# A weight tile's place in memory and the squares of x: two edits to a three-pass fp32r transformer block

## The chip, the cores and the metric

One core of a Trainium2 chip runs the kernel; its other engines are ScalarE (ACT), VectorE (DVE), GpSimd (POOL) and SyncE (SP, which issues transfers) beside TensorE (PE, with its weight loads as PEld). The metric is the device time of one execution in microseconds; three executions are shown. A profile, with its rows, comes from one further execution.

## The reference, cut to what matters

```python
h = rmsnorm(x, norm1_gain)                      # x: 512 positions x 2048
proj = h @ w_in                                 # 2048 x 7176, columns split among head groups
o_a = hgrn2_mixer(q_a, f_a, i_a, g_a, ...)      # 8 heads, chunked gated recurrence
o_b = fox_mixer(q_b, k_b, v_b, f_b, ...)        # 8 heads, forgetting attention
x = x + concatenate([o_a, o_b]) @ w_out         # 2048 x 2048
h = rmsnorm(x, norm2_gain)
x = x + (silu(conv3(h @ w_gate)) * (h @ w_up)) @ w_down    # 2048 x 5632, 5632 x 2048
y = rmsnorm(x, final_norm_gain)
```

The first norm needs, for each position, the sum of the squares of x over all 2048 features.

## The kernel before, in words

Everything is kept transposed: 128 features on the partitions, 512 positions along the row. Each fp32 operand is split into a high part in float32r (ScalarE copies it) and a low part, the rest (VectorE subtracts), and a product is made of three matmuls: high by high, low by high, high by low (`mms`, L211 to L213, and `v_unit`, L294 to L296).

The stages run one after the other. The **mixing stage** multiplies by w_in and runs the heads; the **output projection** multiplies by w_out; the **gate/up stage** multiplies by w_gate and w_up with half-width (256 column) matmuls on sums of quarter blocks (L832 to L834); the **down stage** multiplies by w_down. In the mixing stage, the output projection and the down stage the weights come through one `Stream`: SP loads 512 KB pieces called raw, `make` splits each half of a piece into whi (L159, ScalarE) and wlo (L160, VectorE), 512 columns each, and TensorE uses them in blocks of 128 columns. Two pieces are made ahead of use.

The **head** is the first `v_unit` (L345): its 16 blocks k of 12 matmuls each use one 128-row tile of x per block, loaded and split just before (`load_x`, L278; high part L228 on ScalarE, low part L229 on VectorE). In the head the activations are the stationary operand and the weights the moving one. `before(k)` loads two tiles of x ahead; `after(k)` puts the squares of x into the sum `acc1`: a square on ScalarE (L234 the first, L238 the others) and an addition (L239), which `after` gives to GpSimd. At k = 12 `rms_stats` starts; its matmuls L251 sum `acc1` over the partitions. A square and its addition are written at k = 4 to 11, but the scheduler that lays out each engine's queue issues what is ready first, and x is ready long before.

The heads' own work runs between the products of the projection, as generators that `step()` moves on after each product: per HGRN head four groups of small matmuls (L434; L442 to L452; L464 and L466; L474), per FoX head ten (L599; four times L211 to L213 or L614 on small tiles; four times L633; L656 to L658). `gates` (L573) multiplies by the weights of the forget gates, 40 columns a block, in 32 matmuls L577.

Where a tile lies follows from the order in which pools are opened. On the left lie small tiles, then the activations' pool `pa`, then raw (`wr`) and the weight parts (`wp`); on the right `po`, `px` and the forms of the gate/up stage. Tiles that only fill space set the offsets: `even` (EVEN floats), `even_cm` and `even_sm`, and, in the gate/up stage alone, `shift` (SHIFT = 16 floats, 64 bytes) ahead of the weight parts `wh` (L764, L765). So before the change the weight parts start at multiples of 512 bytes in all stages but gate/up, as the activations do in every stage; in gate/up they start 64 bytes past one.

Of the kernel before, what the change touches and what calls it, by code (L numbers as in the profile page):

```python
# [8 lines left out]
F32 = mybir.dt.float32  # L9
F32R = mybir.dt.float32r  # L10
I32 = mybir.dt.int32
AF = mybir.ActivationFunctionType
ALU = mybir.AluOpType
AX = mybir.AxisListType

P = 128
T = 512
D = 2048
KT = D // P
# [21 lines left out]
LEAD = 2  # L41
DMA_SUMS = True
SHIFT = 16
EVEN = 376
EVEN_CM = 24
EVEN_SM = 40

# [10 lines left out]
def tile_hymba_block(ctx: ExitStack, tc: tile.TileContext, xT, wst, wgu, wdn, wfb, consts, out, out_t):  # L58
    nc = tc.nc
    v, s, pe, gp = nc.vector, nc.scalar, nc.tensor, nc.gpsimd  # L60
# [3 lines left out]
    def opened(name, bufs, side="left", **kw):  # L64
        cm = tc.tile_pool(name=name, bufs=bufs, side=side, reuse_waits="tile", **kw)
        pools[name] = (cm, cm.__enter__())
        return pools[name][1]

    def closed(*names):
        for name in names:  # L70
            pools.pop(name)[0].__exit__(None, None, None)


    cp = opened("cp", 1)
    sm = opened("sm", 2)
    ev = opened("ev", 1)
    ev.tile([P, EVEN_SM], F32, name="even_sm")
    mm = opened("mm", 4, space=bass.MemoryType.PSUM)
    mx = opened("mx", 4, space=bass.MemoryType.PSUM)
    pa = opened("pa", 32)  # L80
    wr = opened("wr", 2)
    wp = opened("wp", 4)

    even = opened("even", 1, "right")
    even.tile([P, EVEN], F32, name="even")
    cm = opened("cm", 1, "right")
# [7 lines left out]
    def O(dt=F32, shape=(P, T)):  # L94
        return po.tile(list(shape), dt, name="ot", tag="o")
# [10 lines left out]
    def f32(ap):  # L106
        return ap.bitcast(F32)
# [28 lines left out]
    class Stream:  # L136
# [7 lines left out]
        def make(self):  # L144
            piece = self.made
            self.made += 1
            r, roff = divmod(piece * PIECE, RAW)
            if roff == 0:
                self.raw = self.wr.tile([P, RAW], F32, name="raw", tag="raw")
                width = PIECE if r == 0 else RAW  # L150
                for c in range(0, RAW, width):
                    nc.sync.dma_start(out=self.raw[:, c:c + width], in_=self.src[r, :, c:c + width])
            if self.pool is None:
                hi = self.wp.tile([P, PIECE], F32R, name="whi", tag="whi")
                lo = self.wp.tile([P, PIECE], F32R, name="wlo", tag="wlo")
            else:
                hi, lo = self.pool(F32R), self.pool(F32R)
            src = self.raw[:, roff:roff + PIECE]
            s.activation(hi, src, AF.Copy)  # L159
            v.tensor_tensor(lo, src, f32(hi), op=ALU.subtract)  # L160
            self.parts[piece] = (hi, lo)

        def piece(self, ahead):
# [11 lines left out]
        def four(self, ahead=AHEAD):  # L175
            hi, lo, _ = self.piece(ahead)
            self.n += 4
            return hi, lo

    ws = Stream(wst, NPIECE_A, wr, wp)  # L180


# [19 lines left out]
    def finish():  # L202
        while side:
            step()
# [27 lines left out]
    def square_acc(acc, src, first, eng=v):  # L232
        if first:
            s.activation(acc, src, AF.Square)  # L234
        else:
            sq = sm.tile([P, T], F32, name="sq", tag="sq")
            sq = sq[:, 0:src.shape[1]]
            s.activation(sq, src, AF.Square)  # L238
            eng.tensor_tensor(acc, acc, sq, op=ALU.add)  # L239
# [36 lines left out]
    acc1 = O()  # L276
# [61 lines left out]
            start(rms_stats([acc1], put1, 7))  # L338

    def after(k):  # L340
        for j in range(max(2 * k - 8, 0), min(2 * k - 6, KT)):
            square_acc(acc1, xs[j], j == 0, gp)

    xs = []
    vts = v_out(v_unit(True))  # L345
# [329 lines left out]
    dr = opened("dr", 1, space=bass.MemoryType.DRAM)  # L675
# [53 lines left out]
    def x1_out(d, ps):  # L729
        t = xr.tile([P, T], F32, name="xr", tag="xr")  # L730
        gp.dma_start(out=t, in_=xT[d * P:(d + 1) * P, :])
        v.tensor_tensor(t, t, ps, op=ALU.add)
        nc.sync.dma_start(out=x1d[d], in_=t)
        square_acc(acc2, t, d == 0)
        g = xr.tile([P, T], F32, name="hg", tag="hg", bufs=2)
        s.activation(g, t, AF.Copy, scale=con[:, C_G2 + d:C_G2 + d + 1])
        hg.append(g)
        if d % 2 and d < KT - 1:
            pair_forms(d // 2, hg[d - 1], hg[d])
# [4 lines left out]
    for d in range(WOPEN, KT):  # L744
        ps = MM()
        unit(ps, range(KT), os_)
        x1_out(d, ps)
    closed("wp", "wr", "pa")
    tl = opened("tl", 1)
    pair_forms(KP - 1, hg[-2], hg[-1])  # L750
    closed("xr")
# [8 lines left out]


    wf = opened("wf", 8)

    sh = opened("sh", 1)  # L764
    sh.tile([P, SHIFT], F32, name="shift")  # L765
    wh = opened("wh", LEAD + 2)
    gt = opened("gt", 1)
    ORDER = ("a11", "s2", "a12", "s3", "s1", "a22", "s4")
# [114 lines left out]
    closed("gt", "wh", "sh", "wf", "tl", "tt")  # L883


    wr = opened("wr", 3)
    wp = opened("wp", 4)
    pq = opened("pq", 81, "right")
# [110 lines left out]
            step()  # L999
        start(norm(i, ps, ys, 6 if i < 3 else 0))  # L1000
    finish()
    closed("pq", "wp", "wr", "even", "dr", "mx", "mm", "ev", "sm", "cp")


def _weights(w_in, w_out, w_gate, w_up, w_down):
# [70 lines left out]
```

## Time and profile before

| | us |
|---|---|
| three executions | 2253.15, 2252.39, 2254.7 (median 2253.15) |
| the profiled execution | 2252.45 |
| its span, first to last instruction | 2250.8 |
| TensorE busy | 2224.2 |
| VectorE busy | 1457.9 |
| ScalarE busy | 940.1 |
| GpSimd busy | 172.6 |

The mean granted clock of TensorE is 0.993 of its full 2.4 GHz. Matmuls overlap, so the duration of one is longer than the distance from its start to the next one's; where the text speaks of spacing, it means that distance. The profiled execution is 0.7 us below the median. The first projection starts at 6.0 us, the gate/up stage about 904 us, the down stage about 1751 us.

### The profile page before, as it was taken

To read this page: it belongs to the slowest core of one execution; us is meant where nothing else is said; L and a number is where in the kernel's file an instruction comes from. 1 tells how busy PE (TensorE), PEld (TensorE's weight loads), DVE (VectorE), ACT (ScalarE), POOL (GpSimd) and SP (SyncE) were. 2 spreads that over 40 slices of the span, in tenths; PEclk is the share of its full clock that TensorE was granted. 3 is DMA by queue.
4 is the path that set the end of the run, shared out by engine and by line. 5 is a ranking of instruction groups with operands and counts; after the bars stand their busy time and mean duration, and the time that the engine had idled before them with its cause. 6 is when DMAs were issued, how large, how long until landed. Compare 5 with 4: busy or idle time off the path is not lost. (4 is left out here: it accounts for less than half of the span.)

```text
span 2250.8 us, 34411 instructions
## 1 busy us (share of the span) xinstructions
PE 2224.2 (99%) x13662; PEld 1976.2 (88%) x13662; DVE 1457.9 (65%) x2194; ACT 940.1 (42%) x1484; POOL 172.6 (8%) x259
## 2 busy tenths in 40 slices
PE   8999999999999999999999999999999999999998
PEld 7888888788888887899999999999999788888886
DVE  6676467646457464888888888888888333333345
ACT  5333233234335354555555555555554222222234
POOL 5000000000000000100000000000000512000000
PEclk9999999999999999999999999999999999999999
DMA  5222222222222353888888888888885955332233
GB/s 179 86 85 76 94 85 89 75 88 81 85 85 75 113 169 129 246 224 222 229 214 222 226 223 224 221 221 224 223 220 145 383 205 201 99 98 99 89 103 113
DMA packets 112210, 352.67 MB, mean 157 GB/s; under 512 B 12816, under 2 KB 19088, under 8 KB 112048
## 3 DMA queue, kind: packets, MB, share of 16 engines
q1 hardware_dynamic: 89568, 272.67, 36.6%
q0 software_dynamic: 22336, 77.67, 15.9%
q8 instruction: 107, 1.75, 0.3%
q14 instruction: 55, 0.45, 0.1%
q10 hardware_dynamic: 144, 0.12, 0.0%
HBM read 318.96 MB, written 31.46 MB: 156 GB/s over the span
## 5 line engine op out<-in xcount | busy, mean ns | idle before, releaser
L160 DVE TENSOR_TENSOR wlo<-raw,whi 128x512 fp32r<-128x512 f32 x453 | 315.2, 697 | 453.8 <-ACT whi L159 415.4
L159 ACT ACTIVATE whi<-raw 128x512 fp32r<-128x512 f32 x453 | 284.5, 630 | 672.2 <-PE mxt L212 307.9
L820 ACT ACTIVATE fhi<-wq 128x1024 fp32r<-128x1024 f32 x308 | 328.0, 1066 | 334.2 <-PE pq L833 286.2
L821 DVE TENSOR_TENSOR flo<-wq,fhi 128x1024 fp32r<-128x1024 f32 x308 | 375.9, 1221 | 51.1 <-ACT fhi L820 50.0
L211 PE MATMUL mmt<-at,whi 128*128 128x512 f32 x896 | 354.7, 396 | 0.0
L213 PE MATMUL mmt<-at,wlo 128*128 128x512 f32 x896 | 349.7, 390 | 0.0
L212 PE MATMUL mmt<-at,whi 128*128 128x512 f32 x896 | 349.3, 390 | 0.0
L211 PE MATMUL mxt<-ot,whi 128*128 128x512 f32 x660 | 258.5, 393 | 3.0 <-ACT whi L159 2.7
L213 PE MATMUL mxt<-ot,wlo 128*128 128x512 f32 x660 | 257.9, 391 | 0.9 <-DVE wlo L160 0.9
L212 PE MATMUL mxt<-ot,whi 128*128 128x512 f32 x660 | 257.7, 391 | 0.2
L213 PEld LDWEIGHTS mmt<-at,wlo 128*128 128x128 f32 x896 | 168.1, 188 | 36.0
L211 PEld LDWEIGHTS mmt<-at,whi 128*128 128x128 f32 x896 | 168.3, 188 | 34.8 <-issue 1.9
L212 PEld LDWEIGHTS mmt<-at,whi 128*128 128x128 f32 x896 | 168.4, 188 | 32.9
L211 PEld LDWEIGHTS mxt<-ot,whi 128*128 128x128 f32 x660 | 124.5, 189 | 30.8 <-ACT whi L159 2.9
L212 PEld LDWEIGHTS mxt<-ot,whi 128*128 128x128 f32 x660 | 124.4, 189 | 27.6 <-DMA ot<-actd 1.6
L213 PEld LDWEIGHTS mxt<-ot,wlo 128*128 128x128 f32 x660 | 124.5, 189 | 26.7 <-DVE wlo L160 1.2
L778 POOL DMA_DIRECT2D wq<-wgu x88 | 75.9, 862 | 747.9 <-DVE flo L821 275.9
L796 DVE TENSOR_TENSOR wq<-wq 128x1024 f32<-128x1024 f32 x88 | 107.5, 1222 | 4.2 <-DMA wq<-wgu 2.6
L296 PE MATMUL mmt<-wlo,at 128*128 128x512 f32 x256 | 101.2, 396 | 3.7 <-DVE wlo L160 3.7
L294 PE MATMUL mmt<-whi,at 128*128 128x512 f32 x256 | 101.6, 397 | 0.9 <-ACT whi L159 0.9
L832 PE MATMUL pq<-b11h,fhi 128*128 128x256 f32 x352 | 98.4, 280 | 3.6 <-ACT fhi L820 3.6
L295 PE MATMUL mmt<-whi,at 128*128 128x512 f32 x256 | 100.7, 393 | 0.0
(303 smaller groups left out, 5032.7 us busy)
## 6 DMA issues: line engine op xcount, KB each, us to landing
wq<-wgu SPq DMA_DIRECT2D x220, 512.0 KB, 4.7
raw<-wst SPq DMA_DIRECT2D x143, 512.0 KB, 3.4
wq<-wgu POOLq DMA_DIRECT2D x88, 512.0 KB, 7.2
raw<-wdn SPq DMA_DIRECT2D x87, 512.0 KB, 3.4
ot<-actd POOLq DMA_DIRECT2D x88, 256.0 KB, 6.1
actd<-ah SPq DMA_DIRECT2D x44, 256.0 KB, 3.7
actd<-al SPq DMA_DIRECT2D x44, 256.0 KB, 3.1
xt<-xT SPq DMA_DIRECT2D x16, 256.0 KB, 5.3
```

Source lines behind the costliest of these rows:

```text
L159: s.activation(hi, src, AF.Copy)
L160: v.tensor_tensor(lo, src, f32(hi), op=ALU.subtract)
L211: pe.matmul(ps, lhsT=a, rhs=xh[:, ts], start=(first and i == 0), stop=False)
L212: pe.matmul(ps, lhsT=a, rhs=xl[:, ts], start=False, stop=False)
L213: pe.matmul(ps, lhsT=b, rhs=xh[:, ts], start=False, stop=(last and i == n - 1))
L294: pe.matmul(pss[i], lhsT=xh[:, ts], rhs=hi, start=(k == 0), stop=False)
L295: pe.matmul(pss[i], lhsT=xl[:, ts], rhs=hi, start=False, stop=False)
L296: pe.matmul(pss[i], lhsT=xh[:, ts], rhs=lo, start=False, stop=(k == KT - 1))
L796: v.tensor_tensor(t, raw[f, x], raw[f, y], op=ALU.add)
L820: s.activation(hi, t, AF.Copy)
L821: v.tensor_tensor(lo, t, f32(hi), op=ALU.subtract)
L832: pe.matmul(ps, lhsT=a, rhs=th, start=(first and j == 0), stop=False, **kw)
```

## The change

Weight parts: `shifted(n)` opens a pool with a tile of n floats that nothing uses. It is now opened after `pa` and ahead of `wr` and `wp` (16 floats, 64 bytes, for the mixing stage and the output projection), as before in the gate/up stage (16 floats), and ahead of `wr` and `wp` of the down stage (8 floats, 32 bytes). EVEN falls by 128 floats, so that all on the right lies 512 bytes higher. The last 44 weight parts of the down stage (`ws.pool = O`) come from the activations' pool and don't move.

Squares: 16 of them at k = 5 to 11, two or three a block, each square and its addition queued behind the last conversion (whi on ScalarE, wlo on VectorE) that was made by then; the addition is VectorE's.

```diff
-EVEN = 376
+SHIFT_D = 8
+EVEN = 248
+    def shifted(n):
+        opened("sh", 1).tile([P, n], F32, name="shift")
...
     pa = opened("pa", 32)
+    shifted(SHIFT)
     wr = opened("wr", 2)
     wp = opened("wp", 4)
...
-            s.activation(hi, src, AF.Copy)
-            v.tensor_tensor(lo, src, f32(hi), op=ALU.subtract)
+            queue_ends[:] = [s.activation(hi, src, AF.Copy),
+                             v.tensor_tensor(lo, src, f32(hi), op=ALU.subtract)]
...
     def after(k):
-        for j in range(max(2 * k - 8, 0), min(2 * k - 6, KT)):
-            square_acc(acc1, xs[j], j == 0, gp)
+        js = range(16 * (k - 5) // 7, 16 * (k - 4) // 7) if 5 <= k < 12 else []
+        if js:
+            with tc.issue_after(queue_ends[0].ins), tc.issue_after(queue_ends[1].ins):
+                for j in js:
+                    square_acc(acc1, xs[j], j == 0)
...
-    closed("wp", "wr", "pa")
+    closed("wp", "wr", "sh", "pa")
...
-    sh = opened("sh", 1)
-    sh.tile([P, SHIFT], F32, name="shift")
+    shifted(SHIFT)
     wh = opened("wh", LEAD + 2)
...
+    shifted(SHIFT_D)
     wr = opened("wr", 3)
     wp = opened("wp", 4)
```

Two places show how the queues change. The first is ScalarE in the head, from behind the first high part of x to the conversion of the third block of weights. Before (at is a high part of x, le belongs to the HGRN bounds, ot and sq are squares, whi_202 is the third block's):

```order
L234 ACTIVATE ot_128<-xt_135 128x512
L159 ACTIVATE whi_144<-raw_141 128x512
L159 ACTIVATE whi_172<-raw_141 128x512
L354 ACTIVATE le_596<-le_596 128x16
L228 ACTIVATE at_162<-xt_160,con_94 128x512
L238 ACTIVATE sq_277<-xt_160 128x512
L228 ACTIVATE at_168<-xt_166,con_94 128x512
L238 ACTIVATE sq_308<-xt_166 128x512
L228 ACTIVATE at_190<-xt_188,con_94 128x512
L228 ACTIVATE at_196<-xt_194,con_94 128x512
L238 ACTIVATE sq_311<-xt_188 128x512
L159 ACTIVATE whi_202<-raw_200 128x512
```

Now the same stretch of ScalarE's queue (whi_206 is the third block's, sel is a small constant):

```order
L365 ACTIVATE le_600<-le_600 128x16
L165 ACTIVATE whi_148<-raw_145 128x512
L165 ACTIVATE whi_176<-raw_145 128x512
L235 ACTIVATE at_166<-xt_164,con_98 128x512
L235 ACTIVATE at_172<-xt_170,con_98 128x512
L235 ACTIVATE at_194<-xt_192,con_98 128x512
L235 ACTIVATE at_200<-xt_198,con_98 128x512
L520 ACTIVATE sel_630<-ident_115 8x8
L521 ACTIVATE sel_630<-ident_115 8x8
L165 ACTIVATE whi_206<-raw_204 128x512
```

Four squares that stood ahead of the third block's whi stand behind it now.

The second place is VectorE in the head, around the conversions of the seventh block and later. Before (at is a low part of x here; no addition stands in this queue):

```order
L160 TENSOR_TENSOR wlo_293<-raw_258,whi_292 128x512
L229 SCALAR_TENSOR_TENSOR at_289<-xt_286,con_94,at_288 128x512
L229 SCALAR_TENSOR_TENSOR at_317<-xt_314,con_94,at_316 128x512
L229 SCALAR_TENSOR_TENSOR at_323<-xt_320,con_94,at_322 128x512
L160 TENSOR_TENSOR wlo_329<-raw_326,whi_328 128x512
```

Now, the additions into acc1 (ot_132) between them:

```order
L166 TENSOR_TENSOR wlo_293<-raw_262,whi_292 128x512
L236 SCALAR_TENSOR_TENSOR at_283<-xt_280,con_98,at_282 128x512
L236 SCALAR_TENSOR_TENSOR at_289<-xt_286,con_98,at_288 128x512
L246 TENSOR_TENSOR ot_132<-ot_132,sq_309 128x512
L236 SCALAR_TENSOR_TENSOR at_315<-xt_312,con_98,at_314 128x512
L236 SCALAR_TENSOR_TENSOR at_321<-xt_318,con_98,at_320 128x512
L166 TENSOR_TENSOR wlo_327<-raw_324,whi_326 128x512
L246 TENSOR_TENSOR ot_132<-ot_132,sq_342 128x512
L246 TENSOR_TENSOR ot_132<-ot_132,sq_345 128x512
```

The first addition comes after the sixth block's wlo (wlo_293), three stand by the seventh; the last of the 15 stands two conversions ahead of the sum over partitions.

## Rows read from the trace of the kernel before

**Rows 1.** The page, busy time of each engine, share of the span, instructions.
```profile
PE 2224.2 (99%) x13662; PEld 1976.2 (88%) x13662; DVE 1457.9 (65%) x2194; ACT 940.1 (42%) x1484; POOL 172.6 (8%) x259
```

**Rows 2.** Busy time by stretches: start:end, us, engines (xcount), granted clock, DMA, GB/s.
```profile
6.00:50.68 44.68, 40.98 (x165) 32.70 (x166) 34.09 (x37) 28.33 (x50) 26.42 (x29) 0.92 0.54 187
14.60:21.40 6.80, 5.47 (x13) 4.31 (x14) 6.80 (x5) 6.27 (x12) 5.75 (x5) 0.50 0.55 196
...
760.00:890.00 130.00, 130.00 (x576) 107.63 (x575) 77.96 (x154) 63.59 (x127) 7.72 (x15) 1.00 0.45 148
920.00:1740.00 820.00, 820.00 (x7237) 820.00 (x7237) 711.39 (x862) 430.85 (x518) 72.96 (x85) 1.00 0.82 219
1790.00:2100.00 310.00, 310.00 (x1370) 256.68 (x1369) 105.42 (x155) 72.06 (x114) 28.85 (x54) 1.00 0.42 148
```

**Rows 3.** Timeline of TensorE in the head: start us, us, what [idle before, releaser].
```profile
6.01 0.50 PE L294 MATMUL mmt<-whi,at 128*128 128x512 f32 x1 [0.90 <-ACT whi L159]
...
12.04 0.39 PE L294 MATMUL mmt<-whi,at 128*128 128x512 f32 x1
15.93 0.79 PE L296 MATMUL mmt<-wlo,at 128*128 128x512 f32 x1 [3.50 <-DVE wlo L160]
16.52 0.63 PE L295 MATMUL mmt<-whi,at 128*128 128x512 f32 x1
...
21.21 0.48 PE L294 MATMUL mmt<-whi,at 128*128 128x512 f32 x1
...
50.69 0.95 PE L251 MATMUL mxt<-ones,ot 128*128 128x1 f32 x8
```

**Rows 4.** Timeline of VectorE in the head.
```profile
9.39 4.71 DVE L229 SCALAR_TENSOR_TENSOR at<-xt,con,at 128x512 fp32r<-128x512 f32 x3
14.03 3.53 DVE L160 TENSOR_TENSOR wlo<-raw,whi 128x512 fp32r<-128x512 f32 x2
...
29.19 1.28 DVE L160 TENSOR_TENSOR wlo<-raw,whi 128x512 fp32r<-128x512 f32 x2
30.39 2.06 DVE L229 SCALAR_TENSOR_TENSOR at<-xt,con,at 128x512 fp32r<-128x512 f32 x3
```

**Rows 5.** Timeline of GpSimd in the head.
```profile
12.26 1.28 POOL L239 TENSOR_TENSOR ot<-ot,sq 128x512 f32<-128x512 f32 x1
...
14.04 4.66 POOL L239 TENSOR_TENSOR ot<-ot,sq 128x512 f32<-128x512 f32 x3
```

**Rows 6.** Groups from 4 to 45 us: shapes, xcount, busy us, mean ns, idle before.
```profile
L239 POOL TENSOR_TENSOR ot<-ot,sq 128x512 f32<-128x512 f32 x15 | 23.6, 1576 | 13.5 <-ACT sq L238 12.9
...
L228 ACT ACTIVATE at<-xt,con 128x512 fp32r<-128x512 f32 x16 | 11.2, 708 | 1.4 <-DMA con<-consts 1.4
L238 ACT ACTIVATE sq<-xt 128x512 f32<-128x512 f32 x15 | 9.2, 620 | 1.4 <-POOL ot L239 1.4
L159 ACT ACTIVATE whi<-raw 128x512 fp32r<-128x512 f32 x15 | 9.1, 624 | 10.6 <-DMA raw<-wst 5.5 <-PE mmt L295 3.3 <-DVE at L229 1.7
```

**Rows 7.** Timeline of TensorE after the small matmuls of the first HGRN head.
```profile
90.30 0.40 PE L212 MATMUL mmt<-at,whi 128*128 128x512 f32 x1
90.54 0.40 PE L213 MATMUL mmt<-at,wlo 128*128 128x512 f32 x1
...
91.01 0.39 PE L212 MATMUL mmt<-at,whi 128*128 128x512 f32 x1
...
92.39 0.39 PE L212 MATMUL mmt<-at,whi 128*128 128x512 f32 x1
```

**Rows 8.** Timeline of TensorE after a wait in the gate/up stage.
```profile
912.82 0.28 PE L832 MATMUL pq<-n2h,fhi 128*128 128x256 f32 x1
...
913.18 1.02 PE L271 MATMUL mxt<-dg,ones 128*128 128x512 f32 x2
```

**Rows 9.** Timeline of TensorE around the matmuls with the gate weights.
```profile
408.47 7.56 PE L577 MATMUL mmt<-at,ot 128*40 128x512 f32 x32
415.86 0.39 PE L294 MATMUL mmt<-whi,at 128*128 128x512 f32 x1
```

More of the change, by code (lines that the diff above doesn't have):

```diff
@@ L178, in four @@
             return hi, lo
+    queue_ends = []
     ws = Stream(wst, NPIECE_A, wr, wp)
@@ L1001, in tile_hymba_block @@
     finish()
-    closed("pq", "wp", "wr", "even", "dr", "mx", "mm", "ev", "sm", "cp")
+    closed("pq", "wp", "wr", "sh", "even", "dr", "mx", "mm", "ev", "sm", "cp")
 def _weights(w_in, w_out, w_gate, w_up, w_down):
```

## The prediction

> **What bounds the kernel now.** I read the page first: TensorE is busy for 2224.2 us, 99% of the span [rows 1], so only what lengthens TensorE's own chain counts. Second, the busy time by stretches [rows 2]. Each stretch divided by its matmuls gives a steady spacing: 820 us for 7237 matmuls in the gate/up stage is 113.3 ns for 256 columns. Twice that, 226.7 ns, is what 512 columns cost: 130 us for 576 in the output projection and 310 us for 1370 in the down stage are 226 ns. The gate/up stage already has its weight parts 64 bytes past the activations, the other two have no offset, and the spacing per column is the same. The exception is the head: 165 matmuls took 44.68 us where 165 x 0.2267 = 37.4 us would do, so 7.3 us are lost there. Part of it ran at a granted clock of 0.50, the 1.2 GHz level [rows 2].
>
> Third, the timeline of TensorE in the head [rows 3]. One matmul starts at 12.04 us and the next at 15.93 us, having waited for the low part wlo of the third block. After this idle time the clock is at 1.2 GHz: from 16.52 to 21.21 us 11 matmuls are 0.43 us apart instead of 0.227. That is 3.7 us of wait and about 2.6 us of slow clock (13 matmuls [rows 2] x 0.2 us); the other 1.0 us are two smaller waits for wlo and slightly wide spacings.
>
> Fourth, why wlo is late. VectorE alone makes two low parts of weights in 1.28 us and three of x in 2.06 us, some 0.69 us each [rows 4]. Between 9.39 and 17.56 us, though, three of x take 4.71 us and two of weights 3.53 us [rows 4], and in those microseconds GpSimd is adding squares [rows 5]. Normal would be 2.06 + 1.28 = 3.34 us; the row sums are 8.24 us. So GpSimd's adds, 15 of 1.58 us mean [rows 6], cost VectorE about 4.9 us up to 17.56 us, and 3.8 us of this lies ahead of the end of the third block's wlo (4.71 - 2.06 of the first three; 14.03 to about 15.9, when TensorE starts, less 0.69 of the next).
>
> **The change part by part.**
>
> Squares to VectorE. The GpSimd adds go (23.6 us of GpSimd work [rows 6]), and with them the stretching. The wlo of the third block would be there 3.8 us earlier, at 12.1 us. Two squares on ScalarE (0.62 us each [rows 6]) and a first one also leave the way of the third block's whi, so VectorE can start it earlier still. TensorE wants that wlo for its 28th matmul, at 6.01 + 27 x 0.227 = 12.1 us. The wait goes, and with no idle time the fall of the clock goes too.
>
> What comes in is 15 adds on VectorE at 0.69 us (a two-input pass over 128x512, like wlo), and 16 squares on ScalarE at a later place. Between block 2 and the sum over partitions at 50.69 us [rows 3], now some 32 us of TensorE time, VectorE must do 11 low parts of x, 13 of weights and 15 adds: 39 x 0.69 = 27 us. ScalarE must do 11 x 0.71 + 13 x 0.62 + 16 x 0.62 = 25.8 us [rows 6]. Both fit, with 5 us to spare, and the adds are queued behind the conversions of their own step, two blocks ahead of need. What would be late next is the sum of squares itself; it has those 5 us. I cost the new adds at nothing; uncovered they would cost at most 15 x 0.69 = 10.4 us. SP's queue keeps its order; GpSimd's two small DMAs lose three adds ahead of them, which nobody waits for.
>
> The first square now stands behind the first whi on ScalarE, not ahead of it, and TensorE's first matmul of the projection, at 6.01 us [rows 3], waits for that whi. This gains at most the square's 0.62 us. I set it against a few wide spacings that will stay, and take nothing. **Term 1: -7.3 us** (ends: -7.9 us, and -3.8 us if the clock still falls and some wait stays).
>
> Weight parts 64 bytes off in mixing stage and output projection. Here the trace shows only one thing that could be a matter of addresses. After each group of small matmuls the products of the projection do not fall back to 0.227 at once: from 90.30 to 92.39 us nine take 2.09 us instead of 2.04, some in pairs of 0.47 [rows 7]. Where weights lie 64 bytes off, in the gate/up stage, three spacings after a wait take 0.36 instead of 0.34 us and it is over [rows 8]. So 0.05 us per group would fall to 0.02. Groups: 4 per head in the HGRN heads (transposes, scores with states, outputs, mean of squares), 10 per head in the FoX heads (gate, four scores, four turns, output): 8 x 14 = 112. Upper end 112 x 0.05 = 5.6 us, lower end nothing. I take 0.03 us on two thirds of the groups, since in the FoX heads the next group often comes before nine products have passed: **term 2: -2.2 us**. I lean to the gate/up row because it is the one place with this very offset.
>
> A rule of the Trainium skill speaks against this term. SBUF — State Buffer, section "SBUF: two separate sides", says that within the engine side only the port pair shared by GpSimd and VectorE makes anyone wait, and that TensorE never does. By it the 64 and 32 bytes are worth nothing and the sum stops at term 1; the wide spacings of [rows 7] would then have a cause other than addresses, and no row here decides that.
>
> Weight parts 32 bytes off in the down stage. Its steady spacing is the 226 ns of [rows 2] and it has some dozen groups of small matmuls: a gain of at most 12 x 0.05 = 0.6 us. No row has this offset throughout. The nearest are 32 matmuls with the gate weights, whose blocks are 160 bytes apart, so that every second one starts 32 bytes past a multiple of 64: from 408.47 to 415.86 us they are 0.231 us apart and never reach 0.227 [rows 9]. For the 3 x 660 products of the down stage that would be 1980 x 0.0042 = +8.3 us. Against it: those loads have 40 columns, not 128, and the offset alternates. I take 0, from -0.6 to +8.3 us.
>
> The other moves: tiles on the right lie 512 bytes higher, alike modulo 512, and their padding shrinks. At the borders of the stages other tiles now share addresses; the built program's orders there do not change. Cost nothing; a first load that waits one product longer would be 24 x 0.113 = 2.7 us on a queue that TensorE may not feel.
>
> Sum: the profiled execution took 2252.45 us, 0.7 below the median of 2253.15. 2252.45 - 7.3 - 2.2 = 2242.95, and on the median **2243.6 us**.
>
> **The rivals.** About 0.2%, 4.5 us, is what a measurement of this kernel can tell from no change.
>
> (a) Addresses are worth nothing; only the head gains: 2253.15 - 7.3 = 2245.9 us. For it: the same spacing per column with and without offset [rows 2]. Against it: the quick recovery in [rows 8], though from few places. This is where the rule of the Trainium skill's page SBUF — State Buffer leads.
>
> (b) The head stays slow. VectorE or ScalarE fall behind through the adds between conversions, or the data of the first blocks come too late, and TensorE idles long enough for the clock to fall again: half the gain, 2253.15 - 3.7 = 2249.5 us, within the bound. Against it: 27 us of work in 32.
>
> (c) The 32 bytes spoil the down stage. If weights at half of 64 bytes keep the matmuls from their steady spacing, every product pays. At 0.231 us [rows 9] it is +8.3 us and the kernel ends at 2252 us, no change; at the 0.235 us of the wide pairs in [rows 7] it is 1980 x 0.0083 = +16.5 us, 2260 us, slower. It decides from a spacing of 0.2267 + (9.5 + 4.5) / 1980 = 0.2338 us on. Against it: a wide spacing has so far followed a disturbance, and hardly any disturb the down stage.
>
> (d) The 32 bytes help the steady spacing itself. 512 columns at 2.4 GHz would be 213.3 ns; the 13.4 ns over that on 1980 products are 26 us, and the time 2217 us. No row goes below 0.226 for 512 columns in a row, at any offset.
>
> **How the numbers follow.** Forecast (both terms) 0.50; (a) 0.28; (b) 0.10; (c) 0.10, of which 0.04 ends within the bound and 0.06 slower; (d) 0.02. Faster by over 0.2% are the forecast, (a), (d) and two of the ten of (b), where more than half of the gain comes: 0.82. Within: eight of (b) and four of (c), 0.12. Slower: 0.06. The range: the low end takes the upper bounds, -7.9 - 5.6 - 0.6, at 2239; the high end holds (a) and most of (b), 2250. Outside are (c), (d) and a little of (b).
>
> **What would show it.** In the changed profile: no adds on GpSimd; VectorE's wlo and low parts of x at 0.7 us throughout the head; the third block's wlo before 12 us; the clock at full level from the first matmul to the output projection's end; the sum over partitions at about 43.1 us instead of 50.69. For term 2: nine products after a group of small matmuls at 0.227 from the second or third on. For the down stage: 226 ns as before. I am wrong if TensorE still waits for wlo past 0.5 us in the head, if the down stage's matmuls per stretch change by over 1%, or if the time ends above 2250 us.

## The result, and the profile after

The changed kernel takes **2274.36 us** (median of four executions, 2273.93 to 2276.82) against 2252.83 us of the kernel before in the same comparison: a ratio of 1.0096, 95% interval [1.0079, 1.0114]. It is slower by 21.5 us. The forecast was 2243.6 us, faster by 9.5; the range of 2239 to 2250 does not hold the result. The profiled execution took 2274.59 us, with a span of 2272.9 us. Some executions of the kernel before and of some kernels below take 2278 to 2288 us, and in each of them that was profiled (e1, e8, e10, e12, e13; none of the kernel before) the gate/up products run at a second spacing; the comparison above has none of them.

TensorE is the bound as before, and it is busy longer: the page's busy times, beside [rows 1].

```profile
PE 2248.6 (99%) x13662; PEld 1974.1 (87%) x13662; DVE 1455.5 (64%) x2209; ACT 940.6 (41%) x1484; POOL 149.2 (7%) x244
```

The same 13662 matmuls cover 24.4 us more. The busy time by stretches of the changed kernel says where; the stretches are those of [rows 2], with the head's end moved to its new place.

```profile
6.00:44.14 38.14, 37.90 (x165) 30.80 (x165) 30.82 (x51) 28.60 (x50) 0.00 (x0) 1.00 0.60 218
14.60:21.40 6.80, 6.80 (x31) 5.58 (x30) 6.49 (x11) 6.52 (x13) 0.00 (x0) 1.00 0.86 333
...
760.00:890.00 130.00, 130.00 (x559) 104.19 (x558) 75.75 (x150) 62.09 (x124) 7.51 (x14) 1.00 0.46 150
...
1790.00:2100.00 310.00, 310.00 (x1331) 249.59 (x1330) 103.02 (x152) 69.56 (x111) 34.74 (x65) 1.00 0.43 154
```

The head needs 38.14 us for its 165 matmuls where it needed 44.68, and between 14.6 and 21.4 us, where 13 matmuls ran at a granted clock of 0.50, 31 now run at 1.00. But the same 130 us of the output projection hold 559 matmuls instead of 576, and the same 310 us of the down stage 1331 instead of 1370, with TensorE busy in all of both stretches and the clock at 1.00. No wait came in there. **A matmul of 512 columns starts later after the one ahead of it**: 130 us / 559 = 0.2326 us and 310 / 1331 = 0.2329. Read start to start in the steady part of these two stages, the mean spacing is 226.7 ns before and 233.3 ns after. The difference, 6.67 ns, is 16 cycles at 2.4 GHz.

The starts of the stages turn that into a balance. First the timeline of TensorE in the changed kernel, then in the kernel before, whose sum over partitions starts at 50.69 us [rows 3].

```profile
5.73 0.51 PE L301 MATMUL mmt<-whi,at 128*128 128x512 f32 x1 [0.41 <-ACT whi L165]
...
44.15 0.39 PE L258 MATMUL mxt<-ones,ot 128*128 128x1 f32 x3
...
913.87 0.58 PE L841 MATMUL pq<-b11h,fhi 128*128 128x256 f32 x1 [3.63 <-ACT fhi L829]
...
1760.34 0.50 PE L218 MATMUL mxt<-ot,whi 128*128 128x512 f32 x1 [2.67 <-ACT whi L165]
```

```profile
904.23 0.58 PE L832 MATMUL pq<-b11h,fhi 128*128 128x256 f32 x1 [3.63 <-ACT fhi L820]
...
1751.25 0.50 PE L211 MATMUL mxt<-ot,whi 128*128 128x512 f32 x1 [2.67 <-ACT whi L159]
```

| stretch | before, us | after, us | difference |
|---|---|---|---|
| start to the sum over partitions | 50.69 | 44.15 | -6.5 |
| from there to the gate/up stage | 853.54 | 869.72 | +16.2 |
| gate/up stage | 847.02 | 846.47 | -0.5 |
| down stage to the end of the span | 499.55 | 512.56 | +13.0 |
| span | 2250.8 | 2272.9 | +22.1 |

The waits at the two borders are the same in both (3.63 and 2.67 us). The gain of the head is there; 29 us came in, all in the stages where the weight parts were moved, and none in gate/up, where they stayed.

The 1980 products of the down stage at 6.67 ns make 13.2 us, which is its loss. The 16.2 us ahead of the gate/up stage have two prices. The 2688 products there with the weights stationary go from a mean of 227.6 ns to 233.3, 15.2 us: between the groups of small matmuls the kernel before runs above its 226.7 ns [rows 7], and the changed one is at 233.3 from the first product on. The 603 products behind the head that have the activations stationary and the weights moving go only from 227.5 to 229.4 ns, 1.1 us. Two rows of the changed kernel, nine spacings apart at the place of [rows 7], show the first kind:

```profile
90.29 0.39 PE L219 MATMUL mmt<-at,whi 128*128 128x512 f32 x1
...
92.39 0.39 PE L219 MATMUL mmt<-at,whi 128*128 128x512 f32 x1
```

A stretch of the second kind, in the kernel before and then in the changed one:

```profile
215.00:250.00 35.00, 35.00 (x156) 28.96 (x155) 13.77 (x18) 10.02 (x15) 0.53 (x1) 1.00 0.30 99
```

```profile
215.00:250.00 35.00, 35.00 (x155) 28.71 (x154) 12.53 (x17) 7.64 (x13) 0.53 (x1) 1.00 0.30 93
```

The head went as its step said. The timeline of VectorE in the changed kernel, where [rows 4] had 3.53 us for two low parts of weights and 4.71 us for three of x:

```profile
9.79 1.48 DVE L236 SCALAR_TENSOR_TENSOR at<-xt,con,at 128x512 fp32r<-128x512 f32 x2
11.66 1.29 DVE L166 TENSOR_TENSOR wlo<-raw,whi 128x512 fp32r<-128x512 f32 x2 [0.39 <-ACT whi L165]
12.87 2.73 DVE L236 SCALAR_TENSOR_TENSOR at<-xt,con,at 128x512 fp32r<-128x512 f32 x4
```

Two take 1.29 us and four 2.73, some 0.7 us each all through. The groups of the changed kernel from 4 to 45 us confirm it and give the price of the new adds:

```profile
L236 DVE SCALAR_TENSOR_TENSOR at<-xt,con,at 128x512 fp32r<-128x512 f32 x16 | 11.5, 748 | 1.5 <-ACT at L235 1.5
L166 DVE TENSOR_TENSOR wlo<-raw,whi 128x512 fp32r<-128x512 f32 x17 | 11.4, 685 | 4.7 <-ACT whi L165 4.7
...
L246 DVE TENSOR_TENSOR ot<-ot,sq 128x512 f32<-128x512 f32 x15 | 10.3, 688 | 0.6
```

The 15 adds cost 10.3 us of VectorE at 0.69 us each, as estimated. TensorE waits for none of them; ScalarE waits once, 0.3 us.

### The profile page after: what moved, and what is told of

It reads as the page before. It is cut to its first block, busy times and chain, and to the rows that moved or that the text cites. A ratio compares the mean times of both kernels' runs of the same rounds, so it can differ in the third digit from the quotient of the medians.

```text
span 2272.9 us, 34406 instructions
## 1 busy us (share of the span) xinstructions
PE 2248.6 (99%) x13662; PEld 1974.1 (87%) x13662; DVE 1455.5 (64%) x2209; ACT 940.6 (41%) x1484; POOL 149.2 (7%) x244
## 4 chain that ended last, share of the span: by engine, by line
PE 95%; DMA 2%; issue 1%; DVE 1%; ACT 0%; POOL 0%; SPq 0%; DVEq 0%; POOLq 0%; ACTq 0%
PE pq L842 11%; PE pq L843 11%; PE pq L841 11%; PE mmt L218 9%; PE mmt L219 9%; PE mmt L220 9%; PE mxt L219 7%; PE mxt L220 7%; PE mxt L218 7%; PE mmt L301 2%; PE mmt L303 2%; PE mmt L302 2%; DMA wq<-wgu 1%; DMA ot<-actd 1%; PE mxt L1006 0%
## 5 line engine op out<-in xcount | busy, mean ns | idle before, releaser
L218 PE MATMUL mmt<-at,whi 128*128 128x512 f32 x896 | 358.6, 400 | 0.0
L219 PE MATMUL mmt<-at,whi 128*128 128x512 f32 x896 | 353.7, 395 | 0.0
L218 PE MATMUL mxt<-ot,whi 128*128 128x512 f32 x660 | 262.6, 399 | 3.8 <-ACT whi L165 2.7
L219 PE MATMUL mxt<-ot,whi 128*128 128x512 f32 x660 | 261.8, 397 | 1.5 <-DMA ot<-actd 1.5
```

The costliest lines, as they stand in the source:

```text
L218: pe.matmul(ps, lhsT=a, rhs=xh[:, ts], start=(first and i == 0), stop=False)
L219: pe.matmul(ps, lhsT=a, rhs=xl[:, ts], start=False, stop=False)
```

## The experiments

Two theories stood after this. **Theory A:** the spacing depends on where the stationary block and the moving operand lie to each other, in bytes; the offset that is good for 256 moving columns is bad for 512. **Rival:** the spacing has to do with absolute places, with the stage, or with the other edit (the squares). e2 to e7, e9 and e15 have one execution each.

### The squares alone, and the offset undone by moving the activations too

e1: the change with the two new offsets taken out.

```diff
-EVEN = 248
+EVEN = 376
-    shifted(SHIFT)      # ahead of wr, wp of the mixing stage
-    shifted(SHIFT_D)
```

> The change without its offsets: weight parts of the mixing stage, output projection and down stage at multiples of 512 bytes as before, squares placed and added as in the change. Theory A (the offset of the weight parts costs 6.6 ns at each 512-column matmul, the squares are the gain): about 6.5 us under the kernel before, 2246 us, with the output projection and the down stage back at 226.7 ns a matmul and the sum over partitions at about 44.2 us. Rival (the later squares themselves cost the time further on): stays above 2260 us.

Seven executions took 2245.3 to 2249.8 us (median 2247.2), where twelve of the kernel before took 2252.4 to 2254.3 (median 2252.8): 5.6 us less. Five more of e1 took 2278.5 to 2281.6 and five of the kernel before 2284.9 to 2287.1; with both kinds in it the ratio, 0.9985 [0.9934, 1.0037], decides nothing. e1's profile shows the sum over partitions at 43.32 us and 226.7 ns in output projection and down stage.

e2: the weights stay at the places of the change, and the activations move by the same bytes.

```diff
-    pa = opened("pa", 32)
     shifted(SHIFT)
+    pa = opened("pa", 32)
...
     shifted(SHIFT_D)
...
+    opened("shr", 1, "right").tile([P, 120], F32, name="shiftr")
     pq = opened("pq", 81, "right")
```

> The change, with the activations moved by the same number of bytes as the weight parts: the pool of the split activations 64 bytes up as well in mixing stage and output projection, the activations of the down stage at 32 modulo 512 as its weight parts. Theory A1 (what counts is the offset between the stationary and the moving operand): the output projection and the down stage return to 226.7 ns, and the time to about 2246 us. Theory A2 (what counts is where the operands lie by themselves, and 64 or 32 past 512 is bad): both stay at 233.3 ns and the time at 2274 us.

2249.59 us, against 2274.4. The stretches of e2, in the output projection, gate/up and down stage:

```profile
780.00:880.00 100.00, 100.00 (x443) 82.81 (x442) 62.25 (x124) 49.97 (x100) 5.90 (x11) 1.00 0.46 153
940.00:1700.00 760.00, 760.00 (x6708) 760.00 (x6707) 659.55 (x799) 397.80 (x480) 68.73 (x80) 1.00 0.84 222
1810.00:2090.00 280.00, 280.00 (x1237) 231.86 (x1236) 95.06 (x140) 65.11 (x103) 15.89 (x30) 1.00 0.39 131
```

443, 6708 and 1237 matmuls are the counts of the kernel before in these stretches; the changed kernel has 430, 6708 and 1202. So the place of the weights alone costs nothing here. What costs is their place relative to the activations.

### Other offsets, stage by stage

e3 takes the 64 bytes out of the gate/up stage as well (all offsets 0); e4 exchanges the two new ones (32 bytes in the mixing stage and output projection, 64 in the down stage); e5 keeps the offsets of the change and puts the squares back to GpSimd and their old place; e9 keeps the 64 bytes and drops the 32.

```diff
e3:  all three calls of shifted taken out
e4: -    shifted(SHIFT)      +    shifted(8)       (mixing stage)
    -    shifted(SHIFT_D)    +    shifted(16)
e5: +        for j in range(max(2 * k - 8, 0), min(2 * k - 6, KT)):
    +            square_acc(acc1, xs[j], j == 0, gp)
e9: -    shifted(SHIFT_D)
```

> Squares as in the change, no offset in any stage, the gate/up stage included, where the weight parts now start at a multiple of 512 bytes too. If an offset of 64 bytes is bad everywhere (A2 in its simplest form), the gate/up stage is no slower than its 113.3 ns a matmul, and the time 2246 us. If what an offset does depends on the number of columns that move (256 there, 512 elsewhere), the gate/up stage becomes slower: by the 16 cycles of 2.4 GHz that the other stages lost, 6.7 ns on 7392 matmuls, 49 us, so 2295 us.

> The change with its two offsets exchanged: 32 bytes in mixing stage and output projection, 64 bytes in the down stage. If any offset but zero breaks the steady spacing of 512-column matmuls, both stages stay at 233.3 ns and the time at 2274 us. If the amount counts, one or both of the spacings differ from 233.3 ns; at 226.7 ns in one of them the time is 13 (down stage) or up to 18 us (the other two) less.

> The offsets of the change alone (64 bytes in the mixing stage and output projection, 32 in the down stage), with the squares of x on GpSimd at the old place. If the loss is the spacing of the matmuls alone and the head is a separate gain: the stretches 780:880 and 1810:2090 hold 430 and 1202 matmuls as in the changed kernel (443 and 1237 before), the sum over partitions comes at about 50.7 us again, and the time is 2274.4 + 6.5 = about 2281 us. If the squares on VectorE had a part in the loss (they delay something behind the head), the time comes out below 2278, and the counts between those of the two kernels.

> The changed kernel without the 32 bytes of the down stage, so 64 bytes in the mixing stage and output projection alone. If each stage pays for its own offset: 430 matmuls in the stretch 780:880, 1237 in a stretch of 280 us within the down stage (226.7 ns each), and 2274.4 - 13.0 = about 2261.4 us, 16 us above the squares alone. If my forecast of a gain from the 64 bytes was right and only the down stage lost, about 2243.6 us.

| run | mixing/output, gate/up, down: bytes | spacing, ns | time, us |
|---|---|---|---|
| before | 0 / 64 / 0 | 226.7 / 113.3 / 226.7 | 2252.8 |
| after | 64 / 64 / 32 | 233.3 / 113.3 / 233.3 | 2274.4 |
| e3 | 0 / 0 / 0 | 226.7 / 120.0 / 226.8 | 2294.26 |
| e4 | 32 / 64 / 64 | 233.3 / 113.3 / 233.3 | 2278.37 |
| e5 | 64 / 64 / 32 | 233.3 / 113.3 / 233.3 | 2282.74 |
| e9 | 64 / 64 / 0 | 233.3 / 113.3 / 226.7 | 2261.11 |

Here are the gate/up stretch of e3 and the two 512-column stretches of e9:

```profile
940.00:1700.00 760.00, 760.00 (x6335) 760.00 (x6335) 629.29 (x756) 375.15 (x454) 64.65 (x75) 1.00 0.79 210
```

```profile
780.00:880.00 100.00, 100.00 (x430) 80.12 (x430) 61.86 (x124) 49.53 (x100) 6.44 (x12) 1.00 0.46 155
1810.00:2090.00 280.00, 280.00 (x1237) 231.82 (x1237) 95.81 (x141) 64.95 (x104) 21.00 (x40) 1.00 0.39 139
```

In e3, 760 us hold 6335 matmuls instead of 6708: at offset 0 the 256-column products pay 6.67 ns each, the same 16 cycles, and 7392 of them make 49 us. So 0 is bad where 64 is good, and the other way round for 512 columns. In e9 the output projection pays (430) and the down stage does not (1237), and the time is 13.3 us under that of the change, as its 13.0 us say. In e5 the sum over partitions is back at 51.08 us, the counts are those of the changed kernel, and the time is 8.4 us over it, 6.9 of them in the head: the two edits add up.

e4 ends 4.0 us over the change. With the weights moving, 32 bytes cost more than 64 do: the stretch of the second kind above holds 152 matmuls in e4, and over all 768 such products the spacing is 233.3 ns against 229.3, or 3.1 us. With the weights stationary 64 bytes cost the full 6.67 ns. So at 64 bytes it also matters which of the two operands lies ahead.

```profile
215.00:250.00 35.00, 35.00 (x152) 28.11 (x151) 13.09 (x17) 8.43 (x14) 0.53 (x1) 1.00 0.29 90
```

### A map of offsets, for 512 columns and for 256

e6 changes the offset within a stage: in the down stage after every ten pieces (120 matmuls), in gate/up after every 19 products (456). e7 is the same with each matmul of the down stage split in two halves of 256 columns. (The list of the down stage in the expectation for e6 is to be read without its 112; the kernel's list is below, in floats of 4 bytes.)

```diff
+OFF_D = (0, 1, 2, 4, 8, 12, 16, 20, 24, 32, 40, 48, 64, 80, 96, 128)
+OFF_G = (0, 2, 4, 6, 8, 12, 16, 20, 24, 28, 32, 36, 40, 48, 56, 64)
+                o = self.offset(piece)       # OFF_D[piece // 10] in the down stage
-                hi = self.wp.tile([P, PIECE], F32R, name="whi", tag="whi")
+                hi = self.wp.tile([P, PIECE + self.pad], F32R, name="whi", tag="whi")[:, o:o + PIECE]
e7: +                    for c in (0, QH):
    +                        pe.matmul(ps[:, c:c + QH], lhsT=w, rhs=x[:, c:c + QH], ...)
```

> Squares as changed, no offset in the mixing stage and output projection. In the down stage the weight parts of every ten pieces in turn (120 matmuls) lie 0, 4, 8, 16, 32, 48, 64, 80, 96, 112, 128, 160, 192, 256, 320, 384 and 512 (without the 112) bytes past their old place, in the gate and up products every 19 products 0 to 256 bytes. If the offset between the stationary block and the moving operand sets the spacing: 226.7 ns per matmul where it is 0 and 233.3 at 32 and 64 in the down stage, 120.0 at 0 and 113.3 at 64 in the gate and up products, steps of one kernel that change where the offset changes, so that the map shows which offsets are good. If the spacing belongs to the kernel as a whole (its layout as such, or the execution), it is one value over the whole stage. With half the offsets bad in both stages the time would lie near 2246 + 6 + 25 = about 2277 us.

> The same map, but every matmul of the down stage split in two of 256 columns each. If the number of moving columns decides which offset is good, the halves behave as the gate and up products: 120.0 ns at offset 0 and 113.3 at 64 bytes. If the stage (its tiles and their places) decides, the halves are good at 0 (113.3 each) and bad at 32 and 64 (116.7 or more). The time itself is not what is asked; with twice the instructions it may be 2260 to 2330 us.

The times are 2289.86 and 2299.34 us. The mean spacing, start to start over the matmuls of each offset (gaps from missing records left out, the first offset of a stage read from its steady part), in ns; 4, 320, 384 and 512 bytes and some of gate/up are left out here:

| bytes | 512 columns, down stage (e6) | 256, gate/up (e6) | 256, halves in the down stage (e7) |
|---|---|---|---|
| 0 | 226.7 | 120.0 | 120.0 |
| 8 | 230.6 | 115.6 | 115.6 |
| 16 | 233.3 | 118.3 | 118.3 |
| 32 | 233.3 | 118.3 | 118.3 |
| 48 | 233.3 | 117.8 | 117.8 |
| 64 | 233.3 | 113.3 | 113.3 |
| 80 | 231.9 | 118.8 | 118.8 |
| 96 | 234.3 | 117.3 | 117.3 |
| 128 | 232.4 | 118.7 | 118.7 |
| 160 | 233.4 | 120.0 | 120.0 |
| 192 | 229.0 | **113.3** | **117.8** |
| 256 | 226.8 | 120.0 | 120.0 |

The stretches of e7 that lie within offsets 0, 64 and 256 (a matmul that reaches over the edge of a stretch counts too, two or three here):

```profile
1801.00:1813.00 12.00, 12.00 (x102) 12.00 (x101) 5.11 (x8) 3.17 (x5) 8.42 (x16) 1.00 1.03 417
...
1958.00:1980.00 22.00, 22.00 (x196) 22.00 (x196) 6.98 (x12) 5.06 (x8) 0.00 (x0) 1.00 0.30 97
2128.00:2152.00 24.00, 24.00 (x202) 24.00 (x202) 7.66 (x12) 5.68 (x9) 0.00 (x0) 1.00 0.31 99
```

Split in halves, the down stage behaves as the gate/up stage does: bad at 0 (102 in 12 us), good at 64 (196 in 22), bad at 256. The last two columns agree at every offset but 192. So the **number of moving columns** decides which offset is good, not the stage, its tiles or its data. Of the offsets tried, 512 columns run at 226.7 ns at 0, 256 and 512 bytes only. None is faster than the kernel before had: its three offsets were already good ones.

### Does the spacing belong to the offset alone?

The two values at 192 bytes did not fit that. e12 puts the whole kernel at offsets that the map shows as good, but new ones: 256, 192 and 256 bytes.

```diff
-SHIFT = 16
-SHIFT_D = 8
+SHIFT = 48
+SHIFT_D = 64
-    shifted(SHIFT)      # mixing stage
+    shifted(SHIFT_D)
```

> The changed kernel with every offset moved to another place that the map of offsets shows as good: 256 bytes in the mixing stage, output projection and down stage, 192 in the gate and up products. If the good places repeat (every 256 bytes from 0 for 512 moving columns, every 128 from 64 for 256), the spacings are 226.7 and 113.3 ns again (443, 6708 and 1237 matmuls in the stretches 780:880, 940:1700 and 1810:2090) and the time is that of the squares alone, about 2246.5 us. If only 0 and 64 are good in a whole kernel, at least one stage pays 6.7 ns per matmul: 2258 us or more.

Missed: 2279.22 us (2278.06 to 2283.64 in ten executions), 26.6 us over the seven executions of the kernel before that took 2252.2 to 2253.3. The stretches of e12:

```profile
780.00:880.00 100.00, 100.00 (x443) 82.84 (x442) 61.43 (x124) 49.67 (x101) 5.91 (x11) 1.00 0.47 153
940.00:1700.00 760.00, 760.00 (x6456) 760.00 (x6455) 638.66 (x769) 382.56 (x462) 66.40 (x77) 1.00 0.81 213
1810.00:2090.00 280.00, 280.00 (x1237) 231.84 (x1236) 95.10 (x140) 65.12 (x103) 32.84 (x62) 1.00 0.44 160
```

The 256 bytes are as good as 0 in both 512-column stages (443, 1237). In gate/up 6456 matmuls in 760 us are 117.8 ns, from the start of its steady run to the end, though the map had 113.3 there. So a stage can settle at either of two spacings at one offset. The gate/up stage kept the one it settled at in every profile. The down stage of e7 did not: at 320 bytes its halves ran at 117.8 ns up to some small matmuls at about 2157 us and at 113.3 ns behind them, from 2171 us on. e13 and e14 tried the way in: squares alone, the first three gate/up products at offset 0 and all others at 64 (e13) or 192 bytes (e14).

```diff
-    shifted(SHIFT)
-        hi = wh.tile([P, FORM], F32R, name="fhi", tag="fhi")
+        o = 0 if g < 3 else 16       # e14: 48
+        hi = wh.tile([P, FORM + 64], F32R, name="fhi", tag="fhi")[:, o:o + FORM]
```

> The squares alone, and the first 3 of the 308 gate and up products with their weight parts at offset 0, all others at 64 bytes. If a stage's spacing is settled once, where its steady run begins, and a step from another offset settles it at the lower value (as in the map of offsets), all executions run the gate and up products at 113.3 ns (6709 matmuls in 940:1700), after 72 matmuls at 120 (0.5 us): about 2246.5 + 0.5 = 2247 us, every execution below 2252. If the way in has no part and the spacing is that of the offset in each execution, some executions come at about 2280 again, as with the squares alone.

> The same with 192 bytes in place of 64. If the way in settles the spacing, 113.3 ns as in the map of offsets and 2247 us, where the kernel with 192 bytes from the first product ran at 117.8 in each execution (6456 matmuls in 940:1700, 2278 to 2284 us). If the offset alone decides, 117.8 ns again, 6456 matmuls and about 2279 us.

The gate/up stretch of e13, then of e14:

```profile
940.00:1700.00 760.00, 760.00 (x6455) 760.00 (x6455) 638.47 (x770) 382.17 (x462) 66.40 (x77) 1.00 0.81 213
```

```profile
940.00:1700.00 760.00, 760.00 (x6709) 760.00 (x6708) 659.14 (x798) 396.73 (x479) 69.12 (x80) 1.00 0.84 222
```

e13 missed: 64 bytes entered from 0 settled at 117.8 ns, and its six executions took 2277.8 to 2282.8 us. e14 came out as expected: 113.3 ns, and **ten executions of 2245.1 to 2248.7 us, median 2246.59**, 6.5 us under the twelve of the kernel before that took 2252.4 to 2254.6 (median 2253.1). The ratio given, 0.9950 [0.9912, 0.9988], is too good: it has two executions of about 2285 us on the side of the kernel before.

So how the kernel is built has a say in which of the two comes: the longer time in ten of ten executions of e12 and six of six of e13, the shorter in ten of ten of e14. The way in is the likely reason, though not by the simple rule that a step settles low. It was not tried by itself: e12 and e14 also differ in the offsets of the 512-column stages and in the padding of the gate/up tiles, and the padding is new in e13 too. At 64 bytes entered directly, the profiles of the kernel before, the change, e2, e4, e5, e9 and e11 show 113.3 ns and those of e1, e8 and e10 117.8, and the executions of e1, one program, split seven to five. What decides there, these runs don't tell.

That opened the failed step again: were the 512-column stages only entered badly? e15 is e14 with the down stage at 0, 32, 64, 192 and 128 bytes, each entered from a settled 0.

```diff
+OFF_D = (0, 8, 8, 8, 0, 16, 16, 16, 0, 48, 48, 0, 32, 32, 0, 0)
+    ws.pad = 128
```

> Squares alone and the gate and up products as in the run before (first 3 products at 0, then 192 bytes); in the down stage the weight parts of ten pieces each (120 matmuls) lie at 0, 32, 32, 32, 0, 64, 64, 64, 0, 192, 192, 0, 128, 128, 0 bytes, so that 32, 64, 192 and 128 are each entered from 0. If for 512 moving columns the offset decides, 233.3 ns at 32 and 64 however they are entered, 226.7 at each 0, and about 2246.6 + 720 x 6.67 ns + some 2 us for 192 and 128 = about 2253.5 us. If the way in decides, as for the gate and up products, 226.7 ns at 32 or 64 too, and about 2247 us.

2254.46 us. Its stretches within 32, 0, 64 and 0 bytes:

```profile
1798.00:1858.00 60.00, 60.00 (x259) 48.31 (x258) 19.77 (x30) 13.29 (x21) 8.05 (x15) 1.00 0.50 186
1868.00:1886.00 18.00, 18.00 (x81) 14.88 (x81) 6.05 (x10) 4.10 (x7) 11.73 (x22) 1.00 0.88 337
1900.00:1960.00 60.00, 60.00 (x259) 48.32 (x258) 20.09 (x30) 13.43 (x22) 0.00 (x0) 1.00 0.27 94
1978.00:1998.00 20.00, 20.00 (x90) 16.57 (x89) 7.00 (x11) 4.94 (x8) 0.54 (x1) 1.00 0.33 111
```

Both 60 us stretches hold 259 matmuls; less the 1.7 that overlap the edges (0.39 us each at 0.233 us apart) that is 233.3 ns. Back at 0 it is 226.7 ns again, and 192 and 128 bytes gave 228.9 and 232.4, as in the map. For 512 columns the offset decides at these places, entered from 0 or not. Another way in would not have spared the change its loss; 0 or 256 bytes would.

### The squares: place or engine?

e8 is e1 again. e10 has the squares at the new place but adds them on GpSimd; e11 adds them on VectorE at the old place. All three have the offsets of the kernel before.

```diff
e10: -                    square_acc(acc1, xs[j], j == 0)
     +                    square_acc(acc1, xs[j], j == 0, gp)
e11: +        for j in range(max(2 * k - 8, 0), min(2 * k - 6, KT)):
     +            square_acc(acc1, xs[j], j == 0)
```

> The squares alone, with the offsets of the kernel before, once more and with more rounds. The head should give 50.7 - 43.3 = 7.4 us and nothing be given back: 2252.8 - 7.4 = about 2245.5 us, 443 and 1237 matmuls in the stretches 780:880 and 1810:2090 as before. If the head's gain is taken back by a later wait, the time stays above 2250.

> The squares alone, later as in the change, but still added on GpSimd. If GpSimd's adds stretch VectorE's subtractions wherever they lie, and that is what the head loses by, the sum over partitions comes at 47 to 50 us and the time is 2249 to 2252. If only the place in the order counts (early adds in the way of the third block's parts), it comes at about 44 us and the time is about 2246.

> The squares alone, added on VectorE but at the old place in the order. If the engine counts and not the place, the sum over partitions comes at 43 to 45 us and the time is about 2246. If the place counts, the early adds (0.7 us each) delay the third block's parts, TensorE waits and runs at the low clock again there, and it comes at 46 to 50 us, 2248 to 2252.

| run | adds | sum over partitions at, us | executions at the shorter spacing, us | their median |
|---|---|---|---|---|
| before | GpSimd, early | 50.69 | 2252.1 to 2254.5 (15 of 18) | 2253.1 |
| e8 | VectorE, later | 43.60 | 2245.4 to 2247.0 (four of six) | 2246.2 |
| e10 | GpSimd, later | 45.54 | 2246.6 to 2249.0 (eight of ten) | 2248.5 |
| e11 | VectorE, early | 44.48 | 2245.3 to 2247.6 (all six) | 2246.6 |

The times of the whole kernel follow the head: 6.9, 4.6 and 6.5 us less than before, where the sum over partitions comes 7.1, 5.2 and 6.2 us earlier. (The ratios, 0.9997, 0.9993 and 0.9954, each with 1 in the interval, mix both spacings of gate/up.) The profiled executions of e8 and e10 have 117.8 ns in gate/up, which lies behind the head. GpSimd's adds stretch VectorE at the later place too: in e10's timeline of VectorE one low part takes 1.78 us, and the one of x behind it as long, where both take 0.7 us in the changed kernel, and GpSimd, whose row is the last one here, is adding squares.

```profile
20.48 1.78 DVE L165 TENSOR_TENSOR wlo<-raw,whi 128x512 fp32r<-128x512 f32 x1
22.18 1.78 DVE L235 SCALAR_TENSOR_TENSOR at<-xt,con,at 128x512 fp32r<-128x512 f32 x1
```

```profile
20.33 6.49 POOL L245 TENSOR_TENSOR ot<-ot,sq 128x512 f32<-128x512 f32 x4 [0.99 <-ACT sq L244]
```

But there it has slack, and TensorE feels it only at the end, where the sum waits for GpSimd's last addition (TensorE of e10, then of e11):

```profile
45.54 1.05 PE L257 MATMUL mxt<-ones,ot 128*128 128x1 f32 x8 [1.36 <-POOL ot L245]
```

```profile
44.48 0.95 PE L257 MATMUL mxt<-ones,ot 128*128 128x1 f32 x8
```

Either half of the edit alone removes most of the loss: 5.2 us of the 7.1 (50.69 to 43.60) by the later place, 6.2 by the engine. Both rivals of this test fall in part. It took early adds **and** GpSimd to make the third block's wlo late enough for the clock to fall: from 14.6 to 21.4 us it is 1.00 in e10 and in e11.

## Why the prediction was wrong

**What bounds the kernel:** right. TensorE's chain is the time: its waits and its clock in the head explain the gain, and the spacing of its matmuls at full clock each loss.

**Term 1 (squares, -7.3 us): right.** The sum over partitions was put at about 43.1 us; with the squares alone it comes at 43.32 (e1) and 43.60 (e8), which is -7.4 and -7.1. In the changed kernel it comes at 44.15; 0.3 us of that are the offset, which the head's 165 products pay at 229.0 ns against 227.0. The clock stays at 1.00, wlo takes 0.69 us, no add is left on GpSimd. The third block's wlo comes at about 12.35 us instead of before 12, and TensorE does not wait for it. Rival (b) falls. Only the cause was told too simply: GpSimd's stretching cost VectorE time at the later place as well, but 5.2 of the 7.1 us that TensorE lost came from the early place (e10).

**Term 2 (64 bytes, -2.2 us): the step that failed.** It read from [rows 8] that the offset of the gate/up stage lets TensorE settle sooner, leaned on that row "because it is the one place with this very offset", and carried it over to matmuls of 512 columns. The row has 256 columns. It could not show that the wide spacings were over, either: its three spacings end at another matmul, L271. At 512 columns the same 64 bytes cost 5.7 ns in the mean of the products with the weights stationary (6.67 where nothing comes between) and 1.9 with the weights moving: +16.2 us up to the gate/up stage, and about 0.3 in the head. The settling that the term asked for came, since the products now have their spacing from the first one on, but it is the wider spacing. The ends given, from nothing to -5.6 us, had no loss in them, though the row showed nothing that ruled one out. The first reading already held a hint: 113.3 and 226.7 ns in [rows 2] were the same per column at *different* offsets, which the text took as a sign that the offset does not matter. It mattered for both, and each had its own good one (e3: +49 us for gate/up at 0).

**The 32 bytes (0, from -0.6 to +8.3 us): mis-sized, beyond its end.** Measured +13.0 us, 1980 products at 6.67 ns = 13.2. The reading of [rows 9] had the right sign, but its rule does not hold: the blocks there lie in steps of 160 bytes, so that 0.231 us is a mean over many offsets, and what counts is not the place modulo 64 (0, 64 and 128 bytes differ in the map). At 32 bytes throughout it is 0.2333.

**The rivals.** (c) had the effect, every product pays, at 0.2333 us just under its own point of decision of 0.2338, and in the mixing stage and output projection as well as in the down stage: with the head's gain, 2253.15 - 7.3 + 13.2 + 16.2 + 0.3 = 2275.6 us, against 2274.4 measured. Its reason, half of 64 bytes, was not it, since 64 cost the same in e4. It had a chance of 0.10 for the down stage and none for the others. (a) and (d) fall: addresses are worth something, and no offset tried runs 512 columns under 226.7 ns. The rule that stood behind (a), from the Trainium skill, SBUF — State Buffer, section "SBUF: two separate sides" (on the engine side only the port pair of GpSimd and VectorE makes anyone wait, TensorE never), does not cover what these runs measure: 226.7 against 233.3 ns by the place of the weight parts alone. Its part on GpSimd and VectorE agrees with e10's 1.78 us beside GpSimd's adds.

**The signs named beforehand** did their work. "I am wrong if the down stage's matmuls per stretch change by over 1%": 1370 became 1331, 2.8% fewer.

## What to carry to other kernels

Where TensorE is the bound, divide stretches at full clock by their matmuls before and after any edit that moves a tile: 16 cycles more per matmul showed here as no wait and no idle time anywhere. Take the effect of an offset from rows with the same number of moving columns and the same operand stationary, and give an unknown one a loss as well as a gain. The version that came out best here keeps the weight parts at 0 bytes for 512 columns, has the squares on VectorE, and enters the gate/up products from offset 0 to 192 (e14, 2246.6 us in ten of ten executions; the squares alone are as fast where gate/up runs at 113.3 ns).

## What the runs showed of the hardware that was not expected

- The spacing of matmuls depends on the bytes between the stationary block and the moving operand: 226.7 to 234.3 ns for 512 columns, 113.3 to 121.9 for 256 (e6; 121.9 at 24 bytes). Moving both operands changes nothing (e2). At 64 bytes the direction counts: 233.3 ns with the weights stationary, 229 with the weights moving. Of the Trainium skill, the page TensorE: Matmul & The Clock Gate, section "Step-by-step: what each phase is for", says that loading the next weights takes no read bandwidth from the running matmul; the spacings differ here while the granted clock is 1.00 and nothing waits. Whether the weight load is the cause was not tried apart.
- The good offset depends on the number of columns: 0, 256 and 512 bytes for 512, 64 for 256, with the same weights in the same stage (e6, e7).
- For 256 columns one offset has two lasting spacings, 113.3 and 117.8 ns, 33 us over the 7392 products (7392 x 4.45 ns). The gate/up stage kept the one it settled at; in e7 the halves at 320 bytes went from the higher to the lower behind other matmuls. For 512 columns no such second value showed at 0, 32 or 64 bytes. What picks the one or the other is open.
